# Cross-covariance attention on one core: other parts for one late store, and the last store in one piece

## The chip, the core and the metric

The kernel runs on one core of a Trainium2 chip. The metric is the device time of one execution in microseconds. Before the change the median of three runs is 128.64 us, the lowest 128.51 and the highest 128.71. Beside these stands one execution taken by the hardware profiler, from which every row below comes.

## The reference

For each of 8 x 12 = 96 heads there are Q, K and V of 512 rows and 64 columns, in float32. The attention is between columns, not rows:

```
Q_norm = Q / (norm of Q over the 512 rows + 1e-10)        # K alike
attn   = einsum('bhnd,bhne->bhde', Q_norm, K_norm)        # 64 x 64 for each head
attn   = softmax over e (exp(attn - max), divided by the sum + 1e-10)
out    = einsum('bhnd,bhde->bhne', V, attn)               # 512 x 64, float32
```

Input is 3 x 12.58 MB and output 12.58 MB. Little is computed for each byte.

## The kernel before

**Units.** A unit is four heads of Q or K: 128 partitions with 16 rows of 64 columns each. There are U = 24 units, taken in S = 12 pairs s, so a pair is eight heads. V goes in W = 6 groups w of sixteen heads.

**Steps of a pair.** Q and K are loaded (`load_qk`, lines 185 to 187) and cast to bf16 side by side; TensorE forms their Gram products, whose diagonal holds the squared norms and whose off-diagonal block holds the raw logits; the norms become factors by logarithm and exponential; the logits are scaled, transposed, put through exp on ScalarE and normalised into a block-diagonal 128 x 128 operand. V is loaded (`load_v`, lines 194 and 196), cast, transposed on TensorE and copied back to SBUF. For each pair, four products `outs(s, x)` multiply V by the normalised attention, and four copies `ocopy(s, x)` (L166 on ScalarE, L168 on VectorE) bring them from PSUM to a tile `so[s, i]`; x = 0 and 1 fill rows 0 to 3 and 4 to 7 (of the 8 in the tile) of `so[s, 0]`, and x = 2 and 3 those of `so[s, 1]`.

**The stores.** Each tile `so[s, i]` is [128 partitions, 2, 8 rows, 64 columns] of float32, 512 KB. `store(s, i)` (lines 198 to 207) writes it to HBM. For each partition and each of the two blocks r, the tile's 8 x 64 numbers are 2 KB in one piece, in SBUF and in HBM alike. There are 24 such stores, issued in the order of (s, i). Two are not made by one DMA before the change:

- `FEW` = (9, 1), the fifth from the end. Its block r = 0 leaves in parts by partition, 0 to 92, 92 to 96 and 96 to 128 (three DMAs, L204), and its block r = 1 in one DMA of 128 partitions (L205).
- (11, 1), the last. It leaves in two DMAs (L207): the first takes rows 0 to 3 of the 8, as soon as copy x = 2 has ended, and the second rows 4 to 7, after copy x = 3. Each is 256 KB, and a partition has four runs of 1 KB in all where the whole store would have two of 2 KB.

**What sets the order.** A planner, the class `Order`, gets every step as a piece: its cost on each engine that may take it, the pieces it comes after, the pieces it must be issued behind, and a rank or due time. It walks through time and fixes in which order each engine issues its pieces. Stores are chained, each behind the one before, so the last store stands at the end of SP's queue, and no other piece waits for it. All loads but two on ScalarE's queue, and all stores, are issued by SP. SP also waits before a DMA until an earlier one, eight transfers back, has landed, since a transfer reports on one of eight semaphores in turn.

**Names used below.** "SP's queue" is the sequence of DMA instructions that SP issues; the page calls the traffic of this queue q1. A DMA is carried by some or all of the core's sixteen DMA engines. "Landing" is the moment at which such an engine reports its share as written. A piece `("sh", 11, 1)` (line 457) is the first half of the last store and `("st", 11, 1)` (line 458) the second.

Of the kernel before, what the change touches and what calls it, by code (L numbers as in the profile page):

```python
# [16 lines left out]
J = T // 2  # L17
# [85 lines left out]
def kernel(  # L103
# [7 lines left out]
    nc = tc.nc  # L111
# [3 lines left out]
    S = U // 2  # L115
# [46 lines left out]
    qk32, v32, vb, qkb, gram, scr, kq, n2, r8, kqs, rq, lg, ex, ab, vps, vt, po, so = ({} for _ in range(18))  # L162
# [32 lines left out]
        else:  # L195
            nc.sync.dma_start(out=o[:, c], in_=i[:, c])

    def store(s, i, k=None):
        rows = slice(None) if k is None else slice(k * (J // 2), (k + 1) * (J // 2))
        o = Of[s // 2, s % 2, i].rearrange("p r (j d) -> p r j d", d=D)  # L200
        if (s, i) == FEW:

            for a, b in ((0, 92), (92, 96), (96, 128)):
                nc.sync.dma_start(out=o[a:b, 0], in_=so[s, i][a:b, 0])  # L204
            nc.sync.dma_start(out=o[:, 1], in_=so[s, i][:, 1])  # L205
            return
        nc.sync.dma_start(out=o[:, :, rows], in_=so[s, i][:, :, rows])  # L207

    def cast_qk(u, x):
        s, r = divmod(u, 2)  # L210
# [137 lines left out]
    for i in range(NB["ab"]):  # L348
        a = const.tile([128, HU, 2 * D], BF16, name=f"ab{i}")
# [9 lines left out]
    X = 1.29  # L359
    R = dict(cq=2.5, gr=2.471, sq=0.756, kq=1, rd=3.457, pw=3.5, sc=1, rq=1.9, lg=5, ex=1.1, nm=2.545, cv=1.165, vt=0.9, vc=1.1, ou=2, oc=0.9)  # L360
    BIAS = dict(sc=-0.6, kq=5, cv=1, vc=-0.3, oc=0.6)
    QK_PACE, V_FROM, V_PACE, ST_LAG = 0.631, 0.0377, 0.7486, 1.5133

    def v_at(v):
        return V_FROM + V_PACE * v / U

    def piece(key, engines, after, behind, rank, fn, *args):
        if key[0] in ("cv", "vc", "oc", "kq", "sc"):
            plan.add(key, engines, after, behind, rank, lambda eng: fn(eng, *args))
        else:  # L370
            plan.add(key, engines, after, behind, rank, lambda eng: fn(*args))

    def back(kind, i, n, *rest):
        return (kind, i - n, *rest) if i - n >= 0 else None
# [17 lines left out]
    for u in range(U):  # L392
        s, r = divmod(u, 2)
# [17 lines left out]
    def turns(w):  # L411
        return [(q, f) for q in range(4) for f in ((0, 1) if w == W - 1 and q >= TAIL else (None,))]
# [29 lines left out]
    for s in range(S):  # L442
        for x in range(4):
            i, k = divmod(x, 2)
            n = 4 * s + x - 2
            wait = [("oc", n // 4, n % 4)] if n >= 0 else []
            order = [("ou", s, x - 1) if x else back("ou", s, 1, 3)]
            piece(("ou", s, x), {"PE": 0.5}, [("vc", s // 2, *t) for t in turns(s // 2) if t[0] // 2 == k] + [("nm", s)] + wait, order, R["ou"] + 0.01 * s, outs, s, x)
            n = 2 * s + i - NB["so"]
            free = [("st", n // 2, n % 2)] if k == 0 and n >= 0 else []  # L450
            order = [("oc", s, x - 1) if x else back("oc", s, 1, 3)]
            piece(("oc", s, x), {"ACT": 0.6, "DVE": (0.68, BIAS["oc"])} if s >= BOTH else {"ACT": 0.6}, [("ou", s, x)] + free, order, R["oc"] + 0.01 * s, ocopy, s, x)
        for i in range(2):
            order = [("st", s, 0) if i else back("st", s, 1, 1)]
            if (s, i) == (S - 1, 1):

                piece(("sh", s, i), {"DMA": 0.67}, [("oc", s, 2)], order, v_at(2 * s + i) + ST_LAG, store, s, i, 0)
                piece(("st", s, i), {"DMA": 0.67}, [("oc", s, 3)], [("sh", s, i)], v_at(2 * s + i) + ST_LAG, store, s, i, 1)
            else:
                piece(("st", s, i), {"DMA": X}, [("oc", s, 2 * i), ("oc", s, 2 * i + 1)], order, v_at(2 * s + i) + ST_LAG, store, s, i)  # L460

    ahead = [loaded(x, 0, r) for r in range(2) for x in range(2)]
    held, passed = [], False
# [40 lines left out]
```

## Time and profile before

| | |
|---|---|
| median of the runs | 128.64 us (128.51 to 128.71, 3 runs) |
| the profiled execution, from its first to its last instruction (span) | 127.0 us |
| median less span | 1.6 us |
| traffic with HBM | 37.75 MB read, 12.58 MB written, 396 GB/s over the span |
| busiest compute engines | VectorE 92.8 us (73%), TensorE 77.7 us (61%), ScalarE 72.5 us (57%) |
| issues of the four DMAs of store (9, 1) | begin at 110.63 (the part of 92), 111.82, 113.12 and 114.40 us |
| issues of the five DMAs after them (L207) | begin from 115.75 to 120.05 us |

The page gives for each engine the busy time as a share of the span, and a row of digits for 40 equal slices of the span, in tenths; the row "DMA" is the mean of the sixteen DMA engines. A waiting instruction on SP's queue is put down to the event that came last before it went on. A table of stretches gives, for each stretch, the busy time of the five engines, the granted clock of TensorE, the share of the DMA engines that is busy (slightly over 1 where consecutive packets overlap) and the GB/s that they moved. The profiled execution's own time is its span; what lies around it is known only as the difference from the median of the other runs.

### The profile page before, as it was taken

To read this page: it belongs to the slowest core of one execution; us is meant where nothing else is said; L and a number is where in the kernel's file an instruction comes from. 1 tells how busy PE (TensorE), PEld (TensorE's weight loads), DVE (VectorE), ACT (ScalarE), POOL (GpSimd) and SP (SyncE) were. 2 spreads that over 40 slices of the span, in tenths; PEclk is the share of its full clock that TensorE was granted. 3 is DMA by queue.
4 is the path that set the end of the run, shared out by engine and by line. 5 is a ranking of instruction groups with operands and counts; after the bars stand their busy time and mean duration, and the time that the engine had idled before them with its cause. 6 is when DMAs were issued, how large, how long until landed. Compare 5 with 4: busy or idle time off the path is not lost.

```text
span 127.0 us, 4887 instructions
## 1 busy us (share of the span) xinstructions
PE 77.7 (61%) x2128; PEld 62.9 (50%) x2128; DVE 92.8 (73%) x141; ACT 72.5 (57%) x220; POOL 36.6 (29%) x40
## 2 busy tenths in 40 slices
PE   0065384894844679858594879566797869680000
PEld 0054372773633568647482668445585748460000
DVE  3354749859899899999885898999999799820000
ACT  4000441569877077786692786794829969972000
POOL 4006307300906903033065212213453361200000
PEclk9999999999998555999958967998559995955555
DMA  4999999999999999999999999999999999999993
GB/s 114 415 434 410 430 410 418 417 437 403 425 426 415 410 419 421 405 415 426 430 410 413 415 421 427 412 419 428 401 413 410 403 402 406 401 405 408 405 366 106
DMA packets 15629, 50.64 MB, mean 399 GB/s; under 512 B 1144, under 2 KB 1656, under 8 KB 14200
## 3 DMA queue, kind: packets, MB, share of 16 engines
q1 hardware_dynamic: 15320, 49.29, 96.4%
q10 hardware_dynamic: 288, 1.05, 2.1%
q8 instruction: 16, 0.26, 0.7%
q14 instruction: 5, 0.04, 0.1%
HBM read 37.75 MB, written 12.58 MB: 396 GB/s over the span
## 4 chain that ended last, share of the span: by engine, by line
DVE 39%; DMA 21%; PE 13%; ACT 11%; issue 4%; POOL 2%; DVEq 0%; SPq 0%; POOLq 0%; ACTq 0%
DMA qk<-in_Q_dram 21%; DVE qkb L213 15%; PE gram L233 9%; DVE scr L240 7%; DVE ab L291 6%; ACT vt L166 4%; DVE vb L168 4%; ACT ex L282 3%; ACT so L166 3%; PE vps L302 3%; DVE n L252 2%; DVE vt L168 2%; DVE so L168 2%; PE po L319 1%; ACT kq L166 1%
## 5 line engine op out<-in xcount | busy, mean ns | idle before, releaser
L233 PE MATMUL gram<-qkb 32*128 32x128 bf16 (+1 forms) x1504 | 35.5, 257 | 23.1 <-DVE qkb L213 9.9
L233 PEld LDWEIGHTS <-qkb 32*128 32x128 bf16 (+1 forms) x1504 | 29.9, 114 | 27.7 <-DVE qkb L213 12.7
L213 DVE CAST qkb<-qk 128x1024 bf16<-128x1024 f32 x48 | 36.4, 780 | 8.5 <-DMA qk<-in_Q_dram 6.9
L170 POOL TENSOR_SCALAR vb<-v 128x1024 bf16<-128x1024 f32 x19 | 21.2, 1129 | 45.5 <-DMA v<-in_V_dram 32.0
L166 ACT COPY so<-po 128x512 f32<-128x512 f32 x45 | 25.0, 593 | 5.2 <-PE po L319 5.0
L166 ACT COPY vt<-vps 128x1024 bf16<-128x1024 bf16 (+1 forms) x18 | 17.8, 989 | 17.4 <-PE vps L302 17.3
L302 PE MATMUL vps<-identb,vb 128*128 128x128 bf16 x192 | 20.2, 262 | 5.8 <-POOL vb L170 3.7
L319 PE MATMUL po<-ab,vt 128*64 128x128 bf16 x384 | 19.3, 242 | 5.2 <-issue 2.7
L263 POOL TENSOR_TENSOR kqs<-kq,r 64x512 f32<-64x512 f32 x12 | 14.0, 1164 | 25.8 <-ACT r L259 13.4
L240 DVE SCALAR_TENSOR_TENSOR scr<-gram,eye 64x512 f32<-64x512 f32 x24 | 16.5, 687 | 4.4 <-PE gram L233 4.1
L302 PEld LDWEIGHTS <-vb 128*128 128x128 bf16 x192 | 14.7, 117 | 10.0 <-POOL vb L170 5.1
L319 PEld LDWEIGHTS <-vt 128*64 128x64 bf16 x384 | 13.8, 121 | 9.2 <-issue 4.6
L282 ACT ACTIVATE ex<-lg,rq 128x64 f32<-128x64 f32 x48 | 14.5, 322 | 2.8 <-PE lg L276 2.7
L166 ACT COPY kq<-gram 64x512 f32<-64x512 f32 x12 | 7.0, 581 | 13.5 <-DVE scr L240 13.4
L291 DVE TENSOR_TENSOR ab<-ex,rinv 64x256 bf16<-64x256 f32 x24 | 13.9, 579 | 0.6
L282 ACT ACTIVATION_READ_ACCUMULATOR ex<-lg,rq 128x1 f32 x48 | 10.2, 213 | 0.0
L168 DVE CAST vb<-v 128x1024 bf16<-128x1024 f32 x5 | 7.6, 1527 | 1.2 <-DMA v<-in_V_dram 1.2
L252 DVE TENSOR_REDUCE n<-scr 128x8 f32<-128x512 f32 x12 | 8.1, 679 | 0.1
L276 PE MATMUL lg<-eye,kqs 64*128 64x64 f32 x48 | 6.4, 259 | 2.6 <-issue 1.5
L168 DVE COPY vt<-vps 128x1024 bf16<-128x1024 bf16 (+1 forms) x8 | 7.9, 1019 | 0.1
L276 PEld LDWEIGHTS lg<-eye,kqs 64*128 64x128 f32 x48 | 4.5, 156 | 4.4 <-issue 2.0
L288 DVE RECIPROCAL rinv<-esum 128x4 f32<-128x4 f32 x12 | 2.1, 171 | 2.8 <-ACT ex L282 2.8
(17 smaller groups left out, 16.0 us busy)
## 6 DMA issues: line engine op xcount, KB each, us to landing
v<-in_V_dram SPq DMA_DIRECT2D x11, 1024.0 KB, 17.1
out_dram<-so SPq DMA_DIRECT2D x22, 512.0 KB, 10.2
qk<-in_Q_dram SPq DMA_DIRECT2D x8, 1024.0 KB, 17.4
qk<-in_K_dram SPq DMA_DIRECT2D x8, 1024.0 KB, 17.1
qk<-in_Q_dram SPq DMA_DIRECT2D x8, 512.0 KB, 12.2
qk<-in_K_dram SPq DMA_DIRECT2D x6, 512.0 KB, 12.5
qk<-in_K_dram ACTq DMA_DIRECT2D x2, 512.0 KB, 7.3
v<-in_V_dram SPq DMA_DIRECT2D x2, 512.0 KB
```

Of the source, the lines that this page charges most:

```text
L166: nc.scalar.copy(o, i)
L168: nc.vector.tensor_copy(o, i)
L170: nc.gpsimd.tensor_scalar(out=o, in0=i, scalar1=1.0, scalar2=0.0, op0=ALU.mult, op1=ALU.add)
L213: nc.vector.tensor_copy(qkb[u][:, :, x * D:(x + 1) * D], qk32[s][:, x, r])
L233: nc.tensor.matmul(gram[s][:, h, r, 0], x, x, start=(t == 0), stop=(t == (T if u < WIDE else J) - 1))
L240: nc.vector.scalar_tensor_tensor(out=scr[s][half], in0=gram[s][half, :, :, 0, half].rearrange("p h r d -> p (h r) d"), scalar=1e-20, in1=e ...
L263: (nc.vector if eng == "DVE" else nc.gpsimd).tensor_tensor(out=kqs[s][HI], in0=kq[s][HI], in1=r8[s][HI, :, None].to_broadcast([D, 2 * HU, ...
L276: nc.tensor.transpose(l[:, h, :], kqs[s][HI, 2 * h:2 * h + 2].rearrange("p r d -> p (r d)"), eye2[HI])
L282: nc.scalar.activation(e[:, h, :], lg[s][:, h, :], AF.Exp, scale=rq[s][:, h:h + 1], accum_out=z[:, h:h + 1])
L291: nc.vector.tensor_tensor(out=a[half, :, half], in0=e[half], in1=ri[half, :, None].to_broadcast([D, HU, D]), op=ALU.mult,)
L302: nc.tensor.transpose(ps[:, c, n, :], vb[w][:, J * c + j].rearrange("p r d -> p (r d)"), identb)
L319: nc.tensor.matmul(po[s, x][e * D:(e + 1) * D, j].rearrange("p r d -> p (r d)"), v, ab[s][:, h, :])
```

## The change

Two things change, both in `store` and the lines that plan it. The second and third part of block r = 0 of store (9, 1) are cut at partition 100 instead of 96, so the parts have 92, 8 and 28 partitions (184, 16 and 56 KB) instead of 92, 4 and 32 (184, 8 and 64 KB). And the last store, (11, 1), is one piece after copies x = 2 and 3, made by one DMA of 512 KB, like the stores before it. No compute step changes.

```diff
-    def store(s, i, k=None):
-        rows = slice(None) if k is None else slice(k * (J // 2), (k + 1) * (J // 2))
+    def store(s, i):
         o = Of[s // 2, s % 2, i].rearrange("p r (j d) -> p r j d", d=D)
         if (s, i) == FEW:
 
-            for a, b in ((0, 92), (92, 96), (96, 128)):
+            for a, b in ((0, 92), (92, 100), (100, 128)):
                 nc.sync.dma_start(out=o[a:b, 0], in_=so[s, i][a:b, 0])
             nc.sync.dma_start(out=o[:, 1], in_=so[s, i][:, 1])
             return
-        nc.sync.dma_start(out=o[:, :, rows], in_=so[s, i][:, :, rows])
+        nc.sync.dma_start(out=o, in_=so[s, i])
...
-            if (s, i) == (S - 1, 1):
-
-                piece(("sh", s, i), {"DMA": 0.67}, [("oc", s, 2)], order, v_at(2 * s + i) + ST_LAG, store, s, i, 0)
-                piece(("st", s, i), {"DMA": 0.67}, [("oc", s, 3)], [("sh", s, i)], v_at(2 * s + i) + ST_LAG, store, s, i, 1)
-            else:
-                piece(("st", s, i), {"DMA": X}, [("oc", s, 2 * i), ("oc", s, 2 * i + 1)], order, v_at(2 * s + i) + ST_LAG, store, s, i)
+            piece(("st", s, i), {"DMA": X}, [("oc", s, 2 * i), ("oc", s, 2 * i + 1)], order, v_at(2 * s + i) + ST_LAG, store, s, i)
```

## The prediction

> **What bounds the kernel now.** I read the page first, then the waits of SP's queue late in the span, the timeline of the end, a table of the end by stretches, and last the DMA traffic in windows of a microsecond or less. The page:
>
> ```profile
> span 127.0 us, 4887 instructions
> ...
> DMA  4999999999999999999999999999999999999993
> ...
> q1 hardware_dynamic: 15320, 49.29, 96.4%
> ```
>
> The sixteen DMA engines are busy from the second slice to the last but one, and SP's queue, q1, alone fills 96.4% of their time. No compute engine passes 73%. So the kernel lasts as long as its transfers, and a change to the order or shape of transfers counts only by what it does to the DMA engine that finishes last. Is that also true at the end, where both edits lie? The timeline of ACT and the waits of SP's queue from 100 us on answer it:
>
> ```profile
> 114.00 1.07 ACT L166 COPY so<-po 128x512 f32<-128x512 f32 x2 [0.24 <-PE po L319]
> ```
>
> ```profile
> SPq L207 <- DMA out_dram<-so: 6.8, 10, 0.9
> ...
> SPq L204 <- DMA out_dram<-so: 2.5, 3, 1.0
> ...
> SPq L205 <- DMA out_dram<-so: 0.9, 1, 0.9
> ```
>
> The last two copies, which the last store needs, end at 114.00 + 1.07 = 115.07 us. The last two DMAs are issued only at 119.58 and 120.05, because SP's queue waits at almost every late store for an earlier transfer to land. The data of the last store lies ready for 4.5 us; waiting for its second half too costs nothing. The table of the end by stretches (last two columns: share of the DMA engines that is busy, GB/s) shows what the final microseconds are:
>
> ```profile
> 116.00:120.00 4.00, 0.00 (x0) 0.00 (x0) 0.00 (x0) 0.00 (x0) 0.00 (x0) 0.50 1.05 405
> 120.00:122.00 2.00, 0.00 (x0) 0.00 (x0) 0.00 (x0) 0.00 (x0) 0.00 (x0) 0.50 1.06 407
> 122.00:123.00 1.00, 0.00 (x0) 0.00 (x0) 0.00 (x0) 0.00 (x0) 0.00 (x0) 0.50 0.92 353
> 123.00:124.00 1.00, 0.00 (x0) 0.00 (x0) 0.00 (x0) 0.00 (x0) 0.00 (x0) 0.50 0.83 307
> 124.00:125.00 1.00, 0.00 (x0) 0.00 (x0) 0.00 (x0) 0.00 (x0) 0.00 (x0) 0.50 0.73 258
> 125.00:125.20 0.20, 0.00 (x0) 0.00 (x0) 0.00 (x0) 0.00 (x0) 0.00 (x0) 0.50 0.20 67
> 125.20:125.80 0.60, 0.00 (x0) 0.00 (x0) 0.00 (x0) 0.00 (x0) 0.00 (x0) 0.50 0.06 20
> ```
>
> Sixteen engines at 407 GB/s are 25.4 GB/s each. From 122 us they run dry one after another, and after 125.2 only 0.06 of the engines is busy: one of sixteen. The DMA traffic from 125.22 to 125.73 us shows it alone:
>
> ```profile
> DMA packets 12, 0.01 MB, mean 22 GB/s; under 512 B 1, under 2 KB 12, under 8 KB 12
> ```
>
> These are eleven packets of 1 KB and one small one in 0.51 us. This one engine sets the end of the kernel; I call it the straggler.
>
> **Who the straggler is.** The trace also records when each DMA engine reports its share of a transfer as landed. The part of 92 partitions (L204) has four such landings, at 118.70, 118.95, 119.30 and 119.94 us; the part of 4 has four, 0.18 us after each of these; the part of 32 and every store of 128 have sixteen. So 92 partitions are dealt to 4 engines, 23 rows of 2 KB each, 4 to the same 4 engines, one each, and 32 to all, two each. The slowest of the four lands at 119.94, 120.13 and 120.30 in the three parts; the other engines are done with the third by 119.69. After it the last landing of each transfer is 120.83, 122.12, 123.41, 124.68, 125.37 and 126.05, steps of about 1.29 for a store of 512 KB and 0.68 for a half, without a gap. The straggler is thus one of the four that carry 23 rows of the part of 92. At the end it is 0.50 us behind the next engine (126.05 against 125.54).
>
> **Part 1, other parts for one half of store (9, 1).** The part of 92 is untouched. The next part goes from 4 to 8 rows; if 8 partitions are dealt to 8 engines, the four have one row each as before, and four more engines get one row that they had not. The last part goes from 32 to 28 rows; dealt to 14 engines it gives two each, so twelve keep their two rows and two engines lose both. For the straggler that is 23 + 1 + 2 = 26 rows before and 26 after: nothing. A 2 KB row takes an engine 2.048 KB / 25.4 GB/s = 0.08 us, so four engines end 0.08 later and two 0.16 earlier. Neither shows, since 0.50 us of the straggler's tail covers them; if that cover were gone (no straggler), the four would cost 0.08 us. The three issues stay three (0.26 to 0.34 us each on SP's queue, which waits there for landings anyway), and nothing later than the last store waits for their landings.
>
> How 28 partitions are dealt no row of this trace shows, and 92 to 4, 4 to 4, 32 to 16 and 128 to 16 fit two rules: the largest divisor up to 16 (28 to 14), or the largest power of two that divides (28 to 4, seven rows each on the four that include the straggler). Bounds for the straggler from these: 0, and 5 rows more = 0.40 us. I take 0: the 92 rows, dealt 23 to each, show that equal shares are kept at any price, and the first rule needs nothing more than that. The Trainium skill (DMA: Bandwidth & Descriptors, "Why a DMA increments its semaphore by 16 and not by 1") says the largest k up to 16 that divides, which would be 14 here; by it the term is 0. In this trace the engines that a short part leaves out are not idle: while the parts of 92 and 4 move, from 116 to 120 us, the table has 405 GB/s, since every engine has later stores queued. The same page's "Rules for kernel authors" speaks against this part: it asks for an outermost dimension that is a multiple of 16, so that all engines work, and by it 8 and 28 should be worse than 32; the sum by it would be a loss that the page doesn't price.
>
> **Part 2, the last store whole.** Two DMAs of 256 KB with rows of 1 KB become one of 512 KB with rows of 2 KB, the form of the store before it. Removed from the straggler: the two steps 0.682 + 0.680 = 1.362 us (from landings at 124.684, 125.366 and 126.046). Added: one step of an ordinary store, 1.286 us (123.408 - 122.122; the next one, 124.684 - 123.408, is 1.276). Difference: -0.08 us, on the path that sets the end. One issue of 0.37 to 0.46 us goes too, off the path: the store is issued where the first half was, 119.58, since that wait is for the store eight transfers back; the straggler reaches it at 124.35, so 4.8 us of queued work hide the issue. Waiting for the second copy is hidden by the 4.5 us named above. After it, from 126.05 to 126.98, the closing steps (L499) stay as they are. The packets say the same: 32 of 1 KB follow each other every 42.3 ns (12 in 0.51 us above), 1.354 us, and 16 of 2 KB take 1.280; the rest is one report fewer. Bounds: 0, if the rate of 1 KB rows were no worse in executions without a profile, and -0.09, the largest difference between these steps (1.362 - 1.276).
>
> **Sum.** 0.00 - 0.08 = -0.08 us on the profiled span of 126.98: 126.90. The median of the runs, 128.64, stands 1.66 above the span; I leave that as it is: 128.64 - 0.08 = 128.56. The limit of what can be told from no change is 0.2%, 0.26 us, so this is no change.
>
> **The rivals.**
> - *Light engines decide.* If in unobserved executions the end is set by one of the two engines that lose two rows, the change is worth 0.16 + 0.08 = 0.24 us: 128.40. For: in the profile twelve engines end within 0.5 us of one another. Against: in the profile the straggler takes part in all three parts, so it isn't one of them, and it is half a microsecond behind all others.
> - *Loaded engines decide.* If one of the four that gain a row sets the end, 0.08 - 0.08 = 0: 128.64. Against: that four of the engines outside the first group land their last share at 122.48 to 124.00, two microseconds early, and an engine with one more row is likely to be of those.
> - *Slower: the 28 rows fall on the straggler.* If partitions are dealt by powers of two, the third part gives four engines seven rows in place of two. Straggler: 5 times 0.08 = 0.40, less 0.08: +0.32 us, 128.96. It decides as soon as any engine's gain in rows passes 1, since that outweighs part 2. For: every count seen (4 and 16) is a power of two. Against: each is also the largest divisor.
>
> The change does move what it names; no step of the hand-made order depends on the last store, so nothing else is reordered.
>
> **How the numbers follow.** Forecast 128.56: 0.79. Light engines 128.40: 0.06. Loaded engines 128.64: 0.04. Powers of two 128.96: 0.08. Something not seen here: 0.03. The runs of before spread 0.1 us either way, so the forecast alone is 128.40 to 128.70; the range takes in the light and the slow case with the unknown deal, 128.35 to 128.97. Faster than 128.38 needs the light case at its full price: 0.06 with the unseen. Slower than 128.90 is the power-of-two case and part of the unseen: 0.09. Same: 0.85.
>
> **What would show it.** Right: the DMA issue list has 16 KB and 56 KB beside 184 KB and one 512 KB store more; the last traffic is again one engine alone, now in 2 KB packets, for about half a microsecond; the span is 126.9. The slower rival shows as four landings of the 56 KB part and a lone tail of 0.9 us; the light one as an end without a lone tail. The forecast is wrong if the straggler of this one profile is an accident of that execution.

## The result, and the profile after

| | before | after |
|---|---|---|
| median of 20 runs | 128.69 us | 128.36 us |
| ratio, 95% interval | | 0.9977 (0.9970 to 0.9984) |
| in time | | -0.30 us (-0.39 to -0.21) |
| span of the profiled execution | 127.0 us | 126.5 us |
| last landing to the end of the span | 0.94 us | 0.83 us |

The forecast was -0.08 us. The change brought more than three times that, still a small gain: its interval lies on both sides of the 0.2% that the prediction took as its bound. The page of the kernel after:

```profile
span 126.5 us, 4885 instructions
...
DMA packets 15359, 50.64 MB, mean 400 GB/s; under 512 B 1130, under 2 KB 1130, under 8 KB 13930
...
q1 hardware_dynamic: 15050, 49.29, 96.5%
```

The transfers bound it as before, and no packet of 1 KB is left: "under 2 KB" now counts the same 1130 as "under 512 B". The list of DMA issues of the kernel after has the new parts and one store of 512 KB more (23 where there were 22):

```profile
out_dram<-so SPq DMA_DIRECT2D x23, 512.0 KB, 10.2
...
out_dram<-so SPq DMA_DIRECT2D x1, 56.0 KB
out_dram<-so SPq DMA_DIRECT2D x1, 16.0 KB
```

The end of the kernel after, in the stretches of the prediction (last two columns: busy share of the DMA engines, GB/s):

```profile
122.00:123.00 1.00, 0.00 (x0) 0.00 (x0) 0.00 (x0) 0.00 (x0) 0.00 (x0) 0.50 0.93 361
123.00:124.00 1.00, 0.00 (x0) 0.00 (x0) 0.00 (x0) 0.00 (x0) 0.00 (x0) 0.50 0.84 324
124.00:125.00 1.00, 0.00 (x0) 0.00 (x0) 0.00 (x0) 0.00 (x0) 0.00 (x0) 0.50 0.66 254
125.00:125.20 0.20, 0.00 (x0) 0.00 (x0) 0.00 (x0) 0.00 (x0) 0.00 (x0) 0.50 0.09 31
125.20:125.80 0.60, 0.00 (x0) 0.00 (x0) 0.00 (x0) 0.00 (x0) 0.00 (x0) 0.50 0.02 7
```

The engines run dry in the same way, and one is again alone at the end, but for a shorter time. The last landing is at 125.70 us instead of 126.05. Of these 0.35 us, 0.26 are there before any changed transfer reaches the four engines that carry the part of 92: the last of their four landings comes at 119.68 instead of 119.94 us. That need not be the change's work: experiment 1, which has the old last store, shows 119.65, and experiment 9, which has the old parts, 119.66. This pair of profiles, 0.45 us apart in span, overstates the change, and the runs must decide.

What the prediction had left "as it is" did change: the time from the last landing to the end. SP closes the program with five instructions (L499, after the change L493), each of which waits for two semaphores. DMAs report in turn on the eight semaphores 100, 102, 103, 104, 105, 107, 108 and 109; the five instructions ask them in another order: 104 and 103, 105 and 102, 107 and 100, 108, 109 (the last two each beside one that no DMA uses). How many of the five still stand after the last landing? First the kernel before, from 126.05 us on, then the kernel after, from 125.70 us on (count, then shortest, median and longest in ns):

```profile
L499 SPq EVENT_SEMAPHORE  x3: 28/28/2643, 123.4 to 126.2; - x3
```

```profile
L493 SPq EVENT_SEMAPHORE  x1: 28/28/28, 125.7 to 125.7; - x1
```

Before, the last half reports on semaphore 100, which the third instruction asks. That one stood waiting for 2.6 us (the 2643 ns) after it had found 107, and two more could only follow after it, at 126.105 and 126.167 us. After, the last store reports on 109, which the fifth asks; the four others have passed during the transfers. SP's waits late in the span, first before, then after, show it as well (total, count and longest in us): three waits, one of them of 3.9 us, became five of at most 1.2.

```profile
SPq L499 <- DMA out_dram<-so: 5.4, 3, 3.9
```

```profile
SPq L493 <- DMA out_dram<-so: 5.5, 5, 1.2
```

These rows entered the argument only after the first four experiments. Those set three theories against each other: A, the prediction's own (the 1 KB packets alone, 0.08 us; a carrier of the 92, one of the four engines with 23 rows of that part, sets the end); B, the two engines spared two rows set the end; C, two DMAs at the end cost more than their packets. For the later ones there were two more: D, the closing waits are worth 0.94 - 0.83 = 0.10 us and the packets 0.08; and E, each DMA more costs, wherever it is.

### The profile page after: what moved, and what is told of

The parts are those of the page before. It is cut to its first block, busy times and chain, and to the rows that moved or that the text cites. A ratio compares the mean times of both kernels' runs of the same rounds, so it can differ in the third digit from the quotient of the medians.

```text
span 126.5 us, 4885 instructions
## 1 busy us (share of the span) xinstructions
PE 78.9 (62%) x2128; PEld 64.2 (51%) x2128; DVE 90.7 (72%) x141; ACT 72.5 (57%) x220; POOL 37.4 (30%) x40
## 2 busy tenths in 40 slices
DMA packets 15359, 50.64 MB, mean 400 GB/s; under 512 B 1130, under 2 KB 1130, under 8 KB 13930
## 4 chain that ended last, share of the span: by engine, by line
DVE 34%; DMA 21%; PE 19%; ACT 10%; issue 5%; POOL 2%; SPq 0%; DVEq 0%; ACTq 0%; POOLq 0%
DMA qk<-in_Q_dram 21%; DVE qkb L212 12%; PE gram L232 12%; DVE scr L239 7%; DVE ab L290 5%; ACT so L166 4%; PE po L318 3%; DVE vb L168 3%; ACT ex L281 3%; PE vps L301 3%; DVE n L251 3%; DVE vt L168 2%; ACT vt L166 2%; DVE so L168 1%; POOL kqs L262 1%
## 5 line engine op out<-in xcount | busy, mean ns | idle before, releaser
L232 PE MATMUL gram<-qkb 32*128 32x128 bf16 (+1 forms) x1504 | 36.9, 262 | 20.3 <-DVE qkb L212 7.1
L232 PEld LDWEIGHTS <-qkb 32*128 32x128 bf16 (+1 forms) x1504 | 31.0, 117 | 24.8 <-DVE qkb L212 8.9
L212 DVE CAST qkb<-qk 128x1024 bf16<-128x1024 f32 x48 | 35.3, 758 | 8.4 <-DMA qk<-in_Q_dram 6.8
L170 POOL TENSOR_SCALAR vb<-v 128x1024 bf16<-128x1024 f32 x19 | 22.0, 1169 | 43.9 <-DMA v<-in_V_dram 39.6
L318 PE MATMUL po<-ab,vt 128*64 128x128 bf16 x384 | 20.8, 252 | 5.1 <-ACT so L166 1.7
L301 PE MATMUL vps<-identb,vb 128*128 128x128 bf16 x192 | 18.4, 247 | 6.5 <-POOL vb L170 4.3
L318 PEld LDWEIGHTS <-vt 128*64 128x64 bf16 x384 | 15.2, 127 | 9.4 <-issue 4.8
L301 PEld LDWEIGHTS <-vb 128*128 128x128 bf16 x192 | 13.5, 110 | 10.2 <-POOL vb L170 5.5
L290 DVE TENSOR_TENSOR ab<-ex,rinv 64x256 bf16<-64x256 f32 x24 | 13.4, 556 | 0.6
L168 DVE CAST vb<-v 128x1024 bf16<-128x1024 f32 x5 | 7.0, 1399 | 1.3 <-DMA v<-in_V_dram 1.3
```

Source lines behind the costliest of these rows:

```text
L168: nc.vector.tensor_copy(o, i)
L170: nc.gpsimd.tensor_scalar(out=o, in0=i, scalar1=1.0, scalar2=0.0, op0=ALU.mult, op1=ALU.add)
L212: nc.vector.tensor_copy(qkb[u][:, :, x * D:(x + 1) * D], qk32[s][:, x, r])
L232: nc.tensor.matmul(gram[s][:, h, r, 0], x, x, start=(t == 0), stop=(t == (T if u < WIDE else J) - 1))
L290: nc.vector.tensor_tensor(out=a[half, :, half], in0=e[half], in1=ri[half, :, None].to_broadcast([D, HU, D]), op=ALU.mult,)
L301: nc.tensor.transpose(ps[:, c, n, :], vb[w][:, J * c + j].rearrange("p r d -> p (r d)"), identb)
```

## The experiments

Each ratio is against the kernel before, run beside it on the same chip. Times from ratios are the ratio less 1, times the median of before in that comparison.

**1. The parts alone.**

```diff
-            for a, b in ((0, 92), (92, 96), (96, 128)):
+            for a, b in ((0, 92), (92, 100), (100, 128)):
```

> Only the parts of store (9, 1) are 92, 8 and 28; the last store stays in halves. Theory A (the end is set by one of the four engines that carry 23 rows; their rows are the same): 0.00 us against before. Theory B (the end is often set by one of the two engines that lose two rows): -0.16 to -0.22 us. Theory C (the gain beyond 0.08 us comes from the last store in halves): 0.00 us. All: the part of 28 lands in 14 shares, the part of 8 in 8.

Measured: 0.9999 (0.9990 to 1.0008), -0.01 us (-0.13 to +0.10). The part of 28 lands in 14 shares, the part of 8 in 8. B falls, and so does the rival of the powers of two. The end takes as long as before, 0.95 us from the last landing: the last half still reports on 100.

**2. The whole last store alone.**

```diff
-        nc.sync.dma_start(out=o[:, :, rows], in_=so[s, i][:, :, rows])
+        nc.sync.dma_start(out=o, in_=so[s, i])
...
-                piece(("sh", s, i), {"DMA": 0.67}, [("oc", s, 2)], order, v_at(2 * s + i) + ST_LAG, store, s, i, 0)
```

> Only the last store is whole; the parts stay 92, 4 and 32. Theory A: -0.08 us against before, by the packets' rate on any engine that ends last. Theory B: -0.08 us too. Theory C (two DMAs at the end cost more without a profile than their packets): -0.30 us.

Measured: 0.9981 (0.9972 to 0.9989), -0.24 us (-0.36 to -0.14). The gain is here, as C has it, and A's -0.08 lies outside the interval. From the last landing to the end: 0.84 us.

**3. Both, once more.** No edit to the changed kernel.

> The changed kernel once more, for a second profile and a comparison on the same chip: -0.30 us against before (-0.21 to -0.39). Theory A: one of the four carriers of 23 rows ends last alone. Theory B: the last engines are close together, or the last is one that had no 92-part share.

Measured: 0.9975 (0.9964 to 0.9986), -0.32 us (-0.46 to -0.18), 0.84 us from the last landing. The engine that lands last is again a carrier of the 92, 0.24 us behind the next.

**4. Two stores in halves.**

```diff
-            if (s, i) == (S - 1, 1):
+            if s == S - 1:
```

(and in the two pieces under it the copies `2 * i` and `2 * i + 1` instead of 2 and 3)

> On the kernel before, the last but one store (11, 0) leaves in halves too, so twice as many DMAs in halves. Theories A and B: +0.08 us by the rate of 1 KB packets. Theory C: +0.2 to +0.3 us.

Measured: 1.0016 (1.0007 to 1.0025), +0.21 us (+0.09 to +0.32). The last half now reports on 102, which the second closing instruction asks, so four of them stand after the last landing of this kernel, from 126.28 us:

```profile
L499 SPq EVENT_SEMAPHORE  x4: 28/28/4020, 122.3 to 126.5; - x4
```

From the last landing to the end it is 1.01 us. (The profiled execution took 129.07 us; the median of this kernel is 128.75.) D, formed after this run, gives 0.08 for the packets and 0.07 for the closing: +0.15, inside the interval; A's +0.08 lies just below it.

**5. Halves kept, the last semaphore moved to the end of the row.** One DMA fewer in front:

```diff
-            for a, b in ((0, 92), (92, 96), (96, 128)):
+            for a, b in ((0, 92), (92, 128)):
```

> The kernel before with two parts (92 and 36 partitions) in place of 92, 4 and 32, last store still in halves. One DMA fewer, so the last half reports on the semaphore that the closing waits ask for last. 36 partitions should go to 12 engines, 3 rows each: the carriers of the 92 keep 26 rows. Theory D (the closing waits ask for the eight semaphores in a fixed order, and each one still to be asked for after the last landing costs 0.05 to 0.06 us; the rest of the gain is the 1 KB packets): -0.10 us against before, last landing to end of the span 0.84 us. Theory E (each DMA more costs, wherever it is): -0.2 us. Theory A alone (packets' rate): 0.00.

Measured: 0.9994 (0.9985 to 1.0004), -0.08 us (-0.19 to +0.05): that fits D's -0.10, but the interval takes in zero and reaches E's -0.2, so by the time alone it is unclear. The profile is not: from the last landing, 126.01 us, one closing instruction is left, and it is 0.83 us to the end, with the last store in halves. So it is not the halves that make the closing longer.

```profile
L499 SPq EVENT_SEMAPHORE  x1: 28/28/28, 126.0 to 126.0; - x1
```

**6, 7, 8. The last store whole, one, four and eight more DMAs before it.** The diff for one; for four the set is (7, 0) to (8, 1), for eight (5, 0) to (8, 1):

```diff
+        if (s, i) in ((8, 0),):
+            for r in range(2):
+                nc.sync.dma_start(out=o[:, r], in_=so[s, i][:, r])
+            return
         nc.sync.dma_start(out=o, in_=so[s, i])
```

> The changed kernel with store (8, 0) as two DMAs, one for each block r, packets as before. One DMA more, so the last store reports on the semaphore that the last half had before. Theory D: -0.09 us against before, last landing to end 0.94 us. Theory E: 0.0 to -0.1 us. Theory A alone: -0.3 us, as the changed kernel.

> The changed kernel with stores (7, 0) to (8, 1) as two DMAs each: four DMAs more, the last store reports on a semaphore that the closing waits ask for first. Theory D: +0.06 us against before (0.25 more than the changed kernel at the end, 0.03 for four more reports on each engine), last landing to end 1.08 us. Theory E: +0.5 us or more. Theory A alone: -0.3 us.

> The changed kernel with stores (5, 0) to (8, 1) as two DMAs each: eight DMAs more, so the last store reports on the same semaphore as in the changed kernel. Theory D: 0.06 us above the changed kernel at most (eight reports), so -0.15 to -0.25 us against before and below the run with four, last landing to end 0.84 us. Theory E: far above the run with four.

Measured: 0.9998 (0.9987 to 1.0009) with one, 1.0027 (1.0013 to 1.0041) with four, 1.0026 (1.0016 to 1.0036) with eight. In time: -0.03 (-0.17 to +0.12), +0.35 (+0.17 to +0.53) and +0.33 us (+0.21 to +0.46). A's -0.3 falls in all three. With one more DMA, D's -0.09 and E both fit. With four and eight, D's times were wrong by 0.3 us and by some 0.5 (+0.06 and -0.15 to -0.25 forecast); E's +0.5 or more lies at the top of the interval with four, and that eight cost no more than four speaks against it. The closing itself went as D has it, up and down again: 0.95, 1.10 and 0.84 us from the last landing. Four more DMAs, with the last store on 104, and eight more, on 109, from the last landing of each kernel on (126.02 and 126.11 us):

```profile
L497 SPq EVENT_SEMAPHORE  x5: 28/28/28, 126.0 to 126.3; - x5
```

```profile
L497 SPq EVENT_SEMAPHORE  x1: 28/28/28, 126.1 to 126.1; - x1
```

But the total did not fall from four to eight as D alone would have it. More DMAs cost something, and it shows later than where they were added. From 116 to 120 us the changed kernel, the one with four more and the one with eight more show, in this order,

```profile
116.00:120.00 4.00, 0.00 (x0) 0.00 (x0) 0.00 (x0) 0.00 (x0) 0.00 (x0) 0.50 1.05 406
```

```profile
116.00:120.00 4.00, 0.00 (x0) 0.00 (x0) 0.00 (x0) 0.00 (x0) 0.00 (x0) 0.50 0.99 358
```

```profile
116.00:120.00 4.00, 0.00 (x0) 0.00 (x0) 0.00 (x0) 0.23 (x1) 0.00 (x0) 0.50 0.98 356
```

Some 50 GB/s are missing over 4 us, or 0.20 MB, what all sixteen engines move in 0.5 us. The early engines ran dry: the first of the sixteen landings of the last store comes at 124.03 and 124.24 us instead of 122.63. And the carriers of the 92 are late before the closing: the last of their four landings of this part comes at 119.99 and 120.09 us instead of 119.68, and the last landing of all, later by as much, at 126.02 and 126.11 instead of 125.70. That SP, which waits for the transfer eight back, kept too little queued with smaller DMAs outstanding is the likely cause, but it is argued; it was not tried by itself.

**9 and 12. The packets alone.** On the kernel before, the last store as its two blocks with rows of 2 KB: the same number of DMAs, the same last semaphore, no packet of 1 KB.

```diff
+        if (s, i) in ((11, 1),):
+            for r in range(2):
+                nc.sync.dma_start(out=o[:, r], in_=so[s, i][:, r])
+            return
```

> The kernel before, but the last store's two DMAs are its two blocks r, with rows of 2 KB, in place of two halves with rows of 1 KB. Same number of DMAs, same semaphore for the last. Theory D (closing waits 0.10 us, 1 KB packets 0.08 us): -0.07 us against before, last landing to end 0.94 us. If two DMAs at the end cost something else: 0.00. If the packets cost more than their rate in the trace: -0.2 us.

> The kernel with the last store in two blocks of 2 KB rows once more, for a narrower interval on the packets' share alone (same number of DMAs and same last semaphore as before). If 1 KB packets cost their rate in the trace: -0.07 us against before, and -0.13 or less from both runs together. If they cost about twice that: -0.15 to -0.20 us in this run too. Last landing to end of the span 0.94 us.

Measured: 0.9985 (0.9975 to 0.9994), -0.19 us (-0.32 to -0.08), and 0.9993 (0.9984 to 1.0002), -0.09 us (-0.21 to +0.03). The closing is 0.94 and 0.95 us, as before. The packets are worth something by themselves, -0.14 us in the mean of the two, though only the first interval excludes zero; the 0.08 of the trace lies inside the first interval at its end and well inside the second, and twice that isn't excluded.

**10 and 11. Fewer rows on the carriers.** The changed kernel with other parts of block r = 0:

```diff
-            for a, b in ((0, 92), (92, 100), (100, 128)):
+            for a, b in ((0, 119), (119, 126), (126, 128)):
```

(in the other kernel 0 to 114, 114 to 122, 122 to 128)

> The changed kernel with parts of 119, 7 and 2 partitions: 17 rows to each of 7 engines, then one more each, then one more to two; the other nine get no row of this block. The carriers have 18 or 19 rows in place of 26, the last eight engines lose two. If one of the carriers of the 92 sets the end, as in all profiles so far: -0.25 to -0.35 us against the changed kernel, -0.5 to -0.65 against before, until the engines with no row set it. If it were the engines without such rows that set the end: -0.1 against the changed kernel.

> The changed kernel with parts of 114, 8 and 6 partitions: 19 rows to each of 6 engines, then one to eight, then one to six. Six engines carry 21 rows, two carry one, eight none. If a carrier of the 92 sets the end: -0.2 to -0.3 us against the changed kernel, less than the run with 119 by about 0.1 us; if the late one of the early engines is among the two new carriers, no more than that run by 0.2 us.

Measured: 1.0045 (1.0032 to 1.0059) and 1.0057 (1.0044 to 1.0071), so +0.58 and +0.73 us: the expectation had the wrong sign. The part of 119 lands in seven shares, at 118.25, 118.52, 118.85, 119.47, 119.79, 120.46 and 120.65 us. In the twelve profiles with a part of 92 its four carriers land within at most 1.38 us of each other, so the last two here, 2.2 and 2.4 us after the first, are most likely among the three new carriers, and were late before they got 17 rows. The part of 8 in the profile after agrees: four of its landings come 0.18 to 0.19 us after those of the 92, and the other four, of the engines that gain a row, at 116.83, 118.64, 119.42 and 119.53 us. So only one of these is clearly early and two are late; that stood in this profile before experiment 10 was planned. The end of the kernel with 119:

```profile
125.20:125.80 0.60, 0.00 (x0) 0.00 (x0) 0.00 (x0) 0.00 (x0) 0.00 (x0) 0.50 0.12 48
125.80:126.50 0.70, 0.00 (x0) 0.00 (x0) 0.00 (x0) 0.00 (x0) 0.00 (x0) 0.50 0.05 18
```

Two engines alone (0.12 of sixteen), one until its last landing at 126.33, the other until 126.50. No version found here beats the changed kernel.

## Why the prediction was right or wrong

**What bounds the kernel: right.** In every profile the compute is over by about 116 us and the end is the last landing and what follows. The last engine in the profile after is a carrier of the 92, as before.

**Part 1: right.** Zero was forecast, -0.01 us (-0.13 to +0.10) measured. That 8 and 28 are no multiples of 16 cost nothing that shows. The straggler's lag behind the next engine, which was to cover the moved rows, was smaller than the 0.50 us read from one execution: 0.20 us in experiment 1, 0.22 in the profile after. The count of engines follows the largest divisor up to 16: 28 partitions landed in 14 shares, 36 in 12, 119 in 7, 114 in 6. This is what the Trainium skill (DMA: Bandwidth & Descriptors, "Why a DMA increments its semaphore by 16 and not by 1") states, and these shares agree with it; the four counts in the trace of before could not tell.

**Part 2: right in direction, too small, by a missing term.** What was on the path and the sign were right. The step that failed is "from 126.05 to 126.98, the closing steps (L499) stay as they are". The change takes one DMA out of the row, so the last store reports on 109 instead of 100, and two closing waits no longer stand behind the last landing: -0.10 us. The prediction had the waits eight transfers back in hand for the issue and didn't ask what the same rotation does at the end. This is the size in the profiles, where the tail can be read by itself; in the runs' time no experiment separates 0.10 us from zero. The fourteen profiles agree without an exception:

| last DMA reports on | asked by the closing instruction | last landing to end |
|---|---|---|
| 109 | 5th | 0.83 to 0.85 us (7 profiles) |
| 100 | 3rd | 0.94 to 0.95 us (5 profiles) |
| 102 | 2nd | 1.01 us |
| 104 | 1st | 1.10 us |

The packets' term was 0.08; experiments 9 and 12 give 0.14 with a spread that takes in 0.08. So it may have been sized too small as well; that isn't settled.

**The sum now.** Parts 0.00, packets -0.08 by the trace, closing -0.10: -0.18 to -0.19 us with the digits kept (0.076 to 0.086 for the packets by the prediction's two steps of an ordinary store, 0.104 for the closing). That is just outside the interval of the first comparison (-0.39 to -0.21), and inside those of experiments 2 and 3, for the last at its very end (-0.36 to -0.14, -0.46 to -0.18). With the packets at the measured 0.14 it is -0.24 and inside all three. Some 0.06 to 0.12 us of the 0.30 stay open. One thing could hold it: the last of the four landings of the 92 part is at 119.91 to 120.09 us in three of the four profiles with the last store in halves (119.65 in the fourth), and at 119.62 to 119.69 in the five where it is whole or in blocks and all before it is as in the kernel before or after. No transfer that differs has reached these engines by then, and there is mostly one profile for a kernel, so this may be chance. The times lean that way: the three are longer executions than their kernel's median (129.07 us against 128.75 in experiment 4, 128.63 against 128.44 in experiment 5; before, the runs listed with a span of 127.0 us took 128.74 to 128.84, the median is 128.69), and the fourth is a shorter one (128.48 against 128.65). So the 1.66 us that the prediction put between span and median set a long execution against a median; single runs stand 1.73 to 1.86 above their own span. It wasn't settled.

**The rivals.** Light engines: fell with experiment 1. The point for them was misread too: by the landings on record, ten engines and not twelve end within 0.5 us of one another (125.07 to 125.54), and the straggler is not among them. Loaded engines: in the two profiles of the changed kernel the end is not theirs, but the argument against them, that they are likely the early ones, was wrong for two of the four, by the part of 8 and by experiment 10. It cost nothing in the change (one row each, 0.08 us, behind a later engine) and 0.6 us in experiment 10, which was built on it. Powers of two: fell.

**The chances.** The case that had the most weight gave the direction. That the time lay in the range is luck: 128.36 is 0.01 us above its lower end, which was put there for the light engines, and these gave nothing; the forecast alone reached down to 128.40. And a chance of 0.06 for a gain beyond 0.26 us was too low. The list of cases held only what the transfers do, and nothing for the 0.94 us behind them.

## What to carry to other kernels

When the last event of a kernel is a transfer, follow it to the end of the span: which instruction waits for it, and which waits stand behind that one. Where DMAs take semaphores in turn and the closing asks them in a fixed order, adding or removing a DMA can move the last one to another place in that order, which is worth up to 0.26 us here. And before rows are shifted to "other" engines, find from the landings of a small part whether the engines that it reaches are early; a sorted list of sixteen landings doesn't say.

## What the runs showed of the hardware

Rows of 1 KB follow each other every 42.3 ns on the engine that is alone at the end of the kernel before, and rows of 2 KB every 80 ns on the one at the end of the kernel after (its last three start at 125.137, 125.217 and 125.297 us). That is 24.2 against 25.6 GB/s: halving a row at this size costs 6% of its transfer. A DMA of 92, 114 or 119 partitions loads 4, 6 or 7 engines alone, with 23, 19 or 17 rows each, while the others go on with what is queued (404 to 407 GB/s from 116 to 120 us where no earlier store is split). The engines' progress differs by 3 us (landings of the last store from 122.63 to 125.70 us in the profile after). And more, smaller DMAs ahead of the end do not always keep sixteen such engines busy: 358 and 356 GB/s instead of 406 in the same 4 us of experiments 7 and 8.
